# A first attention step whose side work keeps its written place on ScalarE and VectorE, with squares of 1024 columns

## The chip, the cores and the metric

The kernel runs on one core of a Trainium2 chip. The metric is the device time in microseconds (us); the time before is 915.18 us, the median of three runs (911.49 to 916.68). The engines are TensorE (PE; PEld is its weight load), VectorE (DVE), ScalarE (ACT), GpSimd (POOL) and SyncE (SP, which here only issues transfers).

## The reference, cut to what matters

One layer: a normalized input times a weight matrix, neighbourhood attention per head on a grid of 8 by 64 tokens, a gate, a second weight matrix, a second norm and the residual. All is float32, with 512 tokens, width 2048 and 16 heads of 128.

```python
h = rms_norm(x, norm_pre)                 # x * rsqrt(mean(x*x) + eps) * gain
q, k, v, z = split(h @ w_in, 4)           # 2048 -> 4 * 2048
o = neighbourhood_attention(q, k, v, rpb) # windows of 8 x 16 tokens, bias rpb
y = (o * silu(z)) @ w_out
out = x + rms_norm(y, norm_post)
```

## The kernel before, in words

**Precision and products.** Every float32 operand is split into two parts in a format that TensorE takes at full rate: `hi`, a rounding made by ScalarE, and `lo`, the rest, made by VectorE (`split_a` L145 for x, `prep` L231 for a tile of W). A product is hi*hi + lo*hi + hi*lo. A tile of W is 128 rows by 512 columns; it is called tile m here, and its parts `hi`m and `lo`m stand in three buffers each (the pool `wp`).

**Steps.** The product with `w_in` is cut into eight steps of two heads. Step 0 (m from 0 to 31, `mm_first` L260) multiplies plainly: 32 tiles of W with 12 matmuls of 512 columns each. Steps 1 to 7 use seven half-size products in place of eight (a Winograd scheme), whose operands are sums of blocks of x. Those sums are made once, while step 0 runs: `sum_x` (L157) makes four differences of 128x256 on VectorE for each k from 0 to 7, and `split_a` then splits the results into the operands N2 (buffers a`k`_2) and N4 with S1 (buffers a`k`_0, from where step 0 reads its own operands until tile 16+k is done).

**The norm.** The scale of a token, `rc`, is applied to the products of step 0 when they leave PSUM (`take_first` L280), so the squares of x may be summed beside the matmuls. `square_x` (L169) loads x in token order and squares it on ScalarE with a running sum. Before, it does so in 16 pieces of 128x512 that alternate between two buffers, whose tags `bm` and `braw` later hold the bias of the first head. For the first quarter of the tokens a piece is loaded as two halves of 64 rows. `rstd` (L180) turns the sums into `rc` (VectorE, then a power on GpSimd).

**What sets the order.** The program is written as one loop over m: `prep(m+2)` (parts of a W tile, and the loads that its buffers free), then the matmuls of tile m, then what the table `beside` holds for m. A scheduler then orders each engine's instructions; it may move an instruction past others that it does not depend on. What goes through the helper `InOrder` (L52) keeps its written place. Before, only a few transfers of the last stage use it (`sync`). Every engine works through its queue strictly in the order that the scheduler fixed, and an instruction that waits holds up all behind it on that engine. The in-order queue of SP issues the loads of W (four buffers `raw`), of xT, of x for the squares and of T (eight tiles for step 1).

**Due times.** Tile m+3 can be rounded to `hi` only when the matmuls of tile m are done, since there are three buffers; it is due when tile m+3 starts, two tiles later.

Of the kernel before, what the change touches and what calls it, by code (L numbers as in the profile page):

```python
# [10 lines left out]
F32 = mybir.dt.float32  # L11
F32R = mybir.dt.float32r
AF = mybir.ActivationFunctionType
ALU = mybir.AluOpType

P = 128
D = 2048
L = 512
# [5 lines left out]
KT = D // P  # L24
# [17 lines left out]
KH = KT // 2  # L42
SLOTS = NPASS * KH
FIRST = 2 * KT
A11, S1, A12, N2, A22, N4, N3 = range(NPASS)
# [17 lines left out]
@with_exitstack  # L63
def na_block(ctx: ExitStack, tc: tile.TileContext, xT, x, gpre, gpost, w_in, w_out, rpb, mask, out):
    nc = tc.nc
    sync = InOrder(tc, nc.sync)
    PSUM = bass.MemoryType.PSUM
    cp = ctx.enter_context(tc.tile_pool(name="cp", bufs=1))
    wp = ctx.enter_context(tc.tile_pool(name="wp", bufs=3))
# [2 lines left out]
    sp = ctx.enter_context(tc.tile_pool(name="sp", bufs=1))  # L72
# [7 lines left out]
    def pair(name):  # L80
        return ap.tile([P, 2, L], F32, tag="c", name=name, bufs=6)
# [27 lines left out]
    part = cp.tile([P, 4, 4], F32, name="part")  # L109
    ms = cp.tile([P, 4], F32, name="ms")  # L110
# [4 lines left out]
    for k in range(KH):  # L115
        for n, ops in enumerate(((A11, N4, S1), (A12, A22), (N2, N3))):
            t = ag.tile([P, len(ops), 2, 256], F32R, tag=f"a{k}_{n}", name=f"a{k}_{n}")
# [13 lines left out]
    X = {}  # L131
# [10 lines left out]
            X[k] = X["c", kk - kk % 2][:, kk % 2, :]  # L142
        nc.sync.dma_start(X[k], xT[k])

    def split_a(k, src, o):  # L145

        t, i = AT[k, o]
        src = src.rearrange("p (a b) -> p a b", b=256)
        hi, lo = t[:, i : i + 2, 0, :], t[:, i : i + 2, 1, :]
        nc.scalar.copy(hi, src)  # L150
        nc.vector.tensor_tensor(lo, src, hi.bitcast(F32), ALU.subtract)  # L151

    def take_x(k):
        nc.scalar.activation(X[k], X[k], AF.Copy, scale=gcol[:, k : k + 1])
        split_a(k % KH, X[k], A11 if k < KH else A12)

    def sum_x(k):  # L157
        x0, x1 = X[k], X[k + KH]
        h0, h1 = slice(0, 256), slice(256, 512)
        nc.vector.tensor_tensor(x1[:, h1], x0[:, h1], x1[:, h1], ALU.subtract)  # L160
        nc.vector.tensor_tensor(x0[:, h1], x0[:, h0], x0[:, h1], ALU.subtract)
        nc.vector.tensor_tensor(x0[:, h0], x0[:, h0], x1[:, h1], ALU.subtract)
        nc.vector.tensor_tensor(x1[:, h0], x1[:, h0], x0[:, h0], ALU.subtract)


    x_v = x.rearrange("(r c) d -> c r d", c=GRID_W)
    out_v = out.rearrange("(r c) d -> c r d", c=GRID_W)

    def square_x(i):  # L169
        j, n = divmod(i, 4)  # L170
        ns = slice(n * L, (n + 1) * L)
        t = sp.tile([P, L], F32, tag=("bm", "braw")[i % 2], name=f"sq{i}")
        if j == 0:
            nc.sync.dma_start(t[0:64, :], x_v[56:64, :, ns])
            nc.sync.dma_start(t[64:128, :], x_v[0:8, :, ns])
        else:
            nc.sync.dma_start(t, x_v[16 * j - 8 : 16 * j + 8, :, ns])
        return lambda: nc.scalar.activation(t, t, AF.Square, accum_out=part[:, j, n : n + 1])

    def rstd():  # L180
        nc.vector.reduce_sum(ms, part, axis=mybir.AxisListType.X)
        nc.vector.tensor_scalar(ms, ms, 1.0 / D, EPS, ALU.mult, ALU.add)
        nc.gpsimd.tensor_tensor(rc, ms, mhalf, ALU.pow)

# [20 lines left out]
    for i, m in enumerate(seq):  # L205
        e = max(m - 6, seq[i - NRAW] if i >= NRAW else 0)
# [334 lines left out]
    def at(m, f, *args):  # L541
        beside.setdefault(m, []).append(lambda: f(*args))
# [55 lines left out]
    pending = {}  # L598

    def begin(i):  # L600
        pending[i] = square_x(i)

    for i in range(16):
        at(10 + i, begin, i)
        at(12 + i, lambda i=i: pending.pop(i)())
    at(8, lambda: nc.gpsimd.dma_start(mask_sb, mask))
    at(28, rstd)
    for j in range(4):
        at(28 + j, take_first, 0, j)
        at(FIRST - 1, take_first, 1, j)  # L610
    for k in range(KH):
        at(KT - 1 + 2 * k, sum_x, k)
        at(KT + 2 * k, lambda k=k: split_a(k, X[k], N2))
        at(KT + 1 + 2 * k, lambda k=k: split_a(k, X[k + KH], N4))


    ms3 = cp.tile([P, 4], F32, name="ms3")
# [55 lines left out]
    for m in range(-AHEAD, N):  # L673
# [10 lines left out]
        else:  # L684
            n, k = divmod(m - NIN, KT)
# [69 lines left out]
```

## Time and profile before

| | before |
|---|---|
| median of three runs | 915.18 us (911.49 to 916.68) |
| the profiled execution | 915.94 us |
| its span | 914.2 us |
| PE busy | 891.9 us, 98% of the span |
| DVE busy | 690.0 us, 75% |
| ACT busy | 536.7 us, 59% |

Busy shares are means over stages. Step 0 is the first 100 us of the span. A row of a timeline gives the start, the duration, the engine, the line of the kernel, the operation, and in brackets how long the engine had stood idle before it and what ended that.

### The profile page before, as it was taken

The page shows a single profiled execution, that of the slowest core. Times are in us where ns is not written, and L with a number is a line of the kernel's source. Part 1 is how long each engine was busy: PE and PEld are TensorE (multiplying, and loading weights), DVE is VectorE, ACT ScalarE, POOL GpSimd, SP SyncE. Part 2 cuts the span into 40 slices and gives each one's busy share as a digit, 9 for nine tenths or more (in the row PEclk, how much of TensorE's full clock was granted, in tenths as well). Part 3 has the DMA queues.
Part 4 walks back from the last instruction along what each step waited for, and adds up shares of the span by engine and source line. Part 5 has one row for each costly group of instructions (what it writes and reads, how often), then busy time and mean ns, then how long its engine had stood idle before and what let it go on. Part 6 is the DMA issues. An engine that isn't in the chain of part 4 may idle for free.

```text
span 914.2 us, 13095 instructions
## 1 busy us (share of the span) xinstructions
PE 891.9 (98%) x4232; PEld 738.8 (81%) x4232; DVE 690.0 (75%) x1280; ACT 536.7 (59%) x1049; POOL 35.9 (4%) x63
## 2 busy tenths in 40 slices
PE   9989999999999999999999999999999899999995
PEld 8867888888888888888888888878887688888884
DVE  4845679897989889888979897979798755232336
ACT  7855666575758565855675577647675655232322
POOL 0001000000000000000000000000011100000004
PEclk9999999999999999999999999999999999999998
DMA  8884346855784777476747765776588532337635
GB/s 269 234 236 132 106 133 216 255 173 170 228 259 136 219 215 258 109 221 215 256 116 236 217 221 149 225 245 192 156 263 255 162 81 75 110 97 203 175 114 184
DMA packets 91637, 171.72 MB, mean 188 GB/s; under 512 B 10656, under 2 KB 10656, under 8 KB 91568
## 3 DMA queue, kind: packets, MB, share of 16 engines
q1 hardware_dynamic: 87840, 159.95, 56.8%
q0 software_dynamic: 3296, 10.41, 4.3%
q8 instruction: 33, 0.54, 0.2%
q10 hardware_dynamic: 432, 0.53, 0.2%
q14 instruction: 36, 0.29, 0.1%
HBM read 162.98 MB, written 7.86 MB: 187 GB/s over the span
## 4 chain that ended last, share of the span: by engine, by line
PE 61%; issue 20%; DMA 4%; DVE 4%; POOL 1%; ACT 1%; DVEq 0%; POOLq 0%; ACTq 0%
DMA raw<-in_w_in 4%; PE u5Y L299 4%; PE u1Y L299 4%; PE u3Y L299 3%; PE u6Y L299 3%; PE u L278 3%; PE u4Y L299 3%; PE u2Y L299 3%; PE u7Y L299 3%; PE u5X L299 2%; PE u3X L299 2%; PE u6X L299 2%; PE u1X L299 2%; PE u7X L299 2%; PE u2Z L299 2%
## 5 line engine op out<-in xcount | busy, mean ns | idle before, releaser
L242 DVE TENSOR_TENSOR lo<-raw,hi 128x512 fp32r<-128x512 f32 x208 | 142.3, 690 | 153.7 <-ACT hi L241 138.1
L241 ACT CAST hi<-t 128x512 fp32r<-128x512 f32 x280 | 170.7, 617 | 108.9 <-DVE t L238 22.9
L241 ACT CAST hi<-raw 128x512 fp32r<-128x512 f32 x208 | 128.3, 620 | 153.6 <-PE y L640 80.3
L242 DVE TENSOR_TENSOR lo<-t,hi 128x512 fp32r<-128x512 f32 x280 | 190.0, 685 | 11.8 <-ACT hi L241 8.3
L640 PE MATMUL y<-hi,g 128*128 128x512 f32 x512 | 160.3, 393 | 0.6 <-DVE e L341 0.6
L238 DVE TENSOR_TENSOR t<-t,raw 128x512 f32<-128x512 f32 x224 | 150.0, 686 | 10.6 <-DMA raw<-in_w_in 9.8
L640 PEld LDWEIGHTS y<-hi,g 128*128 128x128 f32 x512 | 95.8, 189 | 21.9 <-DVE e L341 1.5
L640 PE MATMUL y<-lo,g 128*128 128x512 f32 x256 | 100.4, 392 | 0.0
L278 PE MATMUL u<-hi,a 128*128 128x512 f32 x256 | 65.0, 392 | 5.3 <-ACT hi L241 5.3
L278 PEld LDWEIGHTS u<-hi,a 128*128 128x128 f32 x256 | 47.6, 188 | 17.1 <-ACT hi L241 7.4
L640 PEld LDWEIGHTS y<-lo,g 128*128 128x128 f32 x256 | 48.3, 189 | 10.1 <-DVE lo L242 0.2
L278 PE MATMUL u<-lo,a 128*128 128x512 f32 x128 | 35.3, 390 | 1.1 <-DVE lo L242 1.1
L151 DVE TENSOR_TENSOR a<-x,a 128x512 fp32r<-128x512 f32 x32 | 21.6, 688 | 13.7 <-ACT a L150 13.5
L278 PEld LDWEIGHTS u<-lo,a 128*128 128x128 f32 x128 | 24.0, 188 | 6.5 <-DVE lo L242 1.5
L348 ACT ACTIVATE s<-s,rc 128x512 f32<-128x512 f32 x28 | 20.1, 719 | 13.4 <-DVE s L335 12.7
L299 PE MATMUL u7Y<-hi,a 128*128 128x512 f32 x96 | 26.9, 397 | 0.4 <-ACT hi L241 0.4
L419 DVE TENSOR_TENSOR bm<-braw,mask_sb 128x256 f32<-128x256 f32 x48 | 27.2, 598 | 0.0
L299 PE MATMUL u2Y<-hi,a 128*128 128x512 f32 x96 | 26.8, 396 | 0.0
L299 PE MATMUL u6Y<-hi,a 128*128 128x512 f32 x96 | 26.8, 396 | 0.0
L299 PE MATMUL u1Y<-hi,a 128*128 128x512 f32 x96 | 26.8, 396 | 0.0
L299 PE MATMUL u3Y<-hi,a 128*128 128x512 f32 x96 | 26.8, 396 | 0.0
L299 PE MATMUL u5Y<-hi,a 128*128 128x512 f32 x96 | 26.8, 396 | 0.0
(400 smaller groups left out, 1792.4 us busy)
## 6 DMA issues: line engine op xcount, KB each, us to landing
raw<-in_w_in SPq DMA_DIRECT2D x368, 256.0 KB, 3.1
t<-in_w_in SPq DMA_DIRECT2D x112, 256.0 KB, 4.1
raw<-in_w_out SPq DMA_DIRECT2D x64, 256.0 KB, 2.6
x<-in_xT SPq DMA_DIRECT2D x16, 256.0 KB, 4.1
spare<-in_x SPq DMA_DIRECT2D x16, 256.0 KB, 3.8
graw<-zm POOLq DMA_DIRECT2D x14, 256.0 KB, 4.1
gr<-graw POOLq DMA_DIRECT2D x14, 256.0 KB, 4.6
out<-spare SPq DMA_DIRECT2D x14, 256.0 KB, 2.9
```

Source lines behind the costliest of these rows:

```text
L151: nc.vector.tensor_tensor(lo, src, hi.bitcast(F32), ALU.subtract)
L238: nc.vector.tensor_tensor(T[k], T[k], src, ALU.add)
L241: nc.scalar.copy(hi, src)
L242: nc.vector.tensor_tensor(lo, src, hi.bitcast(F32), ALU.subtract)
L278: nc.tensor.matmul(U[n][j], l, r, start=k == 0 and i == 0, stop=k == KT - 1 and i == 2)
L299: nc.tensor.matmul(U[c][s], l, r, start=p in (0, 1, 4) and k == 0 and n == 0, stop=k == KH - 1 and n == 2, skip_group_check=True,)
L348: nc.scalar.activation(t[:, s, :], t[:, s, :], AF.Copy, scale=rc[:, j + s : j + s + 1])
L419: nc.vector.tensor_tensor(bm[:, i, :].rearrange("p (a b) -> p a b", b=8), rev, mask_sb[:, i, :].unsqueeze(2).to_broadcast([P, 32, 8]), ALU ...
L640: nc.tensor.matmul(Y[n][t], l[:, tsl], r, start=k == 0 and i == 0, stop=k == KT - 1 and i == 2)
```

## The change

The differences of x (`sum_x`), the splits of the later operands and the squares go through `InOrder` on VectorE and ScalarE, and the loads for the squares through `sync`; so they keep their written place behind `prep` of the same m. The splits of step 0's own operands (`take_x`) do not. A square now covers 1024 columns: 8 pieces in place of 16, loaded six or fewer tiles ahead (at m = 6+2i, squared at m = 12+2i) into buffers of the pool of pairs (tag `c`, six buffers) in place of `bm` and `braw`.

```diff
-    sync = InOrder(tc, nc.sync)
+    sync, dve, act = (InOrder(tc, e) for e in (nc.sync, nc.vector, nc.scalar))
...
-    def split_a(k, src, o):
+    def split_a(k, src, o, scalar=None, vector=None):
...
-        nc.scalar.copy(hi, src)
-        nc.vector.tensor_tensor(lo, src, hi.bitcast(F32), ALU.subtract)
+        (scalar or nc.scalar).copy(hi, src)
+        (vector or nc.vector).tensor_tensor(lo, src, hi.bitcast(F32), ALU.subtract)
...
-        nc.vector.tensor_tensor(x1[:, h1], x0[:, h1], x1[:, h1], ALU.subtract)
+        dve.tensor_tensor(x1[:, h1], x0[:, h1], x1[:, h1], ALU.subtract)
...
     def square_x(i):
-        j, n = divmod(i, 4)
-        ns = slice(n * L, (n + 1) * L)
-        t = sp.tile([P, L], F32, tag=("bm", "braw")[i % 2], name=f"sq{i}")
+        j, n = divmod(i, 2)
+        ns = slice(2 * n * L, 2 * (n + 1) * L)
+        t = pair(f"sq{i}")
...
-            nc.sync.dma_start(t, x_v[16 * j - 8 : 16 * j + 8, :, ns])
-        return lambda: nc.scalar.activation(t, t, AF.Square, accum_out=part[:, j, n : n + 1])
+            sync.dma_start(t, x_v[16 * j - 8 : 16 * j + 8, :, ns])
+        return lambda: act.activation(t, t, AF.Square, accum_out=part[:, j, n : n + 1])
...
-        nc.vector.reduce_sum(ms, part, axis=mybir.AxisListType.X)
+        nc.vector.reduce_sum(ms, part[:, :, 0:2], axis=mybir.AxisListType.X)
...
-    for i in range(16):
-        at(10 + i, begin, i)
-        at(12 + i, lambda i=i: pending.pop(i)())
+    for i in range(8):
+        at(6 + 2 * i, begin, i)
+        at(12 + 2 * i, lambda i=i: pending.pop(i)())
...
-        at(KT + 2 * k, lambda k=k: split_a(k, X[k], N2))
-        at(KT + 1 + 2 * k, lambda k=k: split_a(k, X[k + KH], N4))
+        at(KT + 2 * k, lambda k=k: split_a(k, X[k], N2, act, dve))
+        at(KT + 1 + 2 * k, lambda k=k: split_a(k, X[k + KH], N4, act, dve))
```

The order of TensorE's instructions is the same in both. On the other engines it differs in step 0 and at the start of step 1 only. ScalarE in the second half of step 0, before (`sq` is a square, `hi` the first part of a tile of W, `a` an operand of step 0 or of a later step):

```order
L178 ACTIVATE sq6_585,part_109<-sq6_585 128x512
L241 CAST hi16_516<-raw16_419 128x512
L150 CAST a6_2_131<-x6_260 128x2x256
L178 ACTIVATE sq7_608,part_109<-sq7_608 128x512
L150 CAST a7_2_134<-x6_260 128x2x256
L241 CAST hi17_537<-raw17_445 128x512
L178 ACTIVATE sq8_635,part_109<-sq8_635 128x512
L178 ACTIVATE sq9_658,part_109<-sq9_658 128x512
L241 CAST hi18_562<-raw18_471 128x512
L241 CAST hi19_589<-raw19_498 128x512
```

ScalarE at the same tiles of W, now (L60 is the helper `InOrder`):

```order
L241 CAST hi16_513<-raw16_425 128x512
L60 ACTIVATE sq1_391,part_109<-sq1_391 128x1024
L241 CAST hi17_534<-raw17_450 128x512
L241 CAST hi18_556<-raw18_473 128x512
L60 ACTIVATE sq2_441,part_109<-sq2_441 128x1024
L60 CAST a0_2_113<-x0_147 128x2x256
L241 CAST hi19_583<-raw19_499 128x512
L60 CAST a0_0_111<-x8_305 128x2x256
L241 CAST hi20_607<-raw20_517 128x512
```

Before, two squares could stand ahead of one part of W, and the operands a6_2 and a7_2 were split while tile 16 was prepared; now each part of W comes first, and one or two pieces of side work follow it. VectorE near the start of the program (`lo` is the second part of a tile of W, `bm` the bias of the first head), before:

```order
L242 TENSOR_TENSOR lo4_233<-raw4_168,hi4_232 128x512
L151 TENSOR_TENSOR a3_0_120<-x3_188,a3_0_120 128x2x256
L242 TENSOR_TENSOR lo5_255<-raw5_177,hi5_254 128x512
L151 TENSOR_TENSOR a4_0_123<-x4_215,a4_0_123 128x2x256
L151 TENSOR_TENSOR a5_0_126<-x4_215,a5_0_126 128x2x256
```

And now:

```order
L242 TENSOR_TENSOR lo4_233<-raw4_168,hi4_232 128x512
L419 TENSOR_TENSOR bm0_924<-braw0_922,mask_sb_103 128x256 x2
L151 TENSOR_TENSOR a3_0_120<-x3_188,a3_0_120 128x2x256
L419 TENSOR_TENSOR bm0_924<-braw0_922,mask_sb_103 128x256
L242 TENSOR_TENSOR lo5_255<-raw5_177,hi5_254 128x512
```

The bias of the first head, whose buffers no square uses any more, moved ahead of the fourth and fifth tiles; its load (`braw0`, on GpSimd's queue) now follows the load of the mask there. SP's queue, where the loads of the first square stood behind x10 to x13 (the blocks of xT for tiles 10 to 13), now reads:

```order
L143 DMA x9_328<-in_xT 128x512
L60 DMA sq0_342<-in_x 64x1x1024
L221 DMA raw10_281<-in_w_in 128x512
L60 DMA sq0_342<-in_x 64x1x1024
L221 DMA raw11_303<-in_w_in 128x512
L143 DMA x10_354<-in_xT 128x512
L143 DMA x11_377<-in_xT 128x512
L221 DMA raw12_326<-in_w_in 128x512
```

So x10 and x11 are issued behind raw11, and 512 KB of squares are ahead of them.

## Rows read from the trace of the kernel before

**Rows 1.** Windows of step 0 and of the rest; columns: stretch, length, busy times.

```profile
5.76:46.74 40.98, 40.98 (x181) 33.86 (x182) 29.89 (x60) 32.06 (x60) 0.00 (x0) 1.00 0.83 256
46.74:76.08 29.34, 23.22 (x97) 17.45 (x95) 13.28 (x28) 16.96 (x40) 1.81 (x2) 1.00 0.76 211
78.94:100.70 21.76, 21.76 (x98) 18.02 (x97) 9.72 (x15) 8.06 (x14) 0.58 (x1) 1.00 0.43 119
100.70:914.20 813.50, 798.71 (x3825) 662.87 (x3823) 633.51 (x1174) 473.66 (x928) 31.91 (x50) 0.99 0.61 186
```

**Rows 2.** Timeline of PE in step 0: first matmuls of some tiles of W.

```profile
46.74 0.61 PE L278 MATMUL u<-hi,a 128*128 128x512 f32 x2
...
58.72 2.12 PE L278 MATMUL u<-hi,a 128*128 128x512 f32 x8 [1.40 <-ACT hi L241]
...
76.08 2.11 PE L278 MATMUL u<-hi,a 128*128 128x512 f32 x8 [1.90 <-ACT hi L241]
...
78.94 1.98 PE L278 MATMUL u<-hi,a 128*128 128x512 f32 x8
```

**Rows 3.** Who waited for whom from 46 to 78 us: total, times, longest.

```profile
ACT sq L178 <- DMA sq<-in_x: 11.1, 9, 1.9
...
PE u L278 <- ACT hi L241: 5.0, 4, 1.9
...
ACT c L285 <- POOL rc L183: 1.7, 1, 1.7
```

**Rows 4.** Timeline of ACT before one of PE's stops.

```profile
55.69 0.63 ACT L178 ACTIVATE sq<-sq 128x512 f32<-128x512 f32 x1 [1.42 <-DMA sq<-in_x]
...
57.44 0.63 ACT L178 ACTIVATE sq<-sq 128x512 f32<-128x512 f32 x1 [1.03 <-DMA sq<-in_x]
...
58.07 1.12 ACT L241 CAST hi<-raw 128x512 fp32r<-128x512 f32 x2
```

**Rows 5.** Groups by line, 0 to 115 us: busy, mean ns, idle before.

```profile
L242 DVE TENSOR_TENSOR lo<-raw,hi 128x512 fp32r<-128x512 f32 x32 | 22.0, 690 | 24.1 <-ACT hi L241 17.5 <-PE u L278 6.4 <-issue 0.2
...
L241 ACT CAST hi<-raw 128x512 fp32r<-128x512 f32 x32 | 19.6, 616 | 8.6 <-PE u L278 5.8 <-DMA raw<-in_w_in 2.6
...
L178 ACT ACTIVATE sq<-sq 128x512 f32<-128x512 f32 x16 | 10.1, 631 | 14.8 <-DMA sq<-in_x 14.7
...
L163 DVE TENSOR_TENSOR x<-x,x 128x256 f32<-128x256 f32 x8 | 3.4, 420 | 0.0
...
L178 ACT ACTIVATION_READ_ACCUMULATOR sq<-sq 128x1 f32 x16 | 3.0, 187 | 0.0
```

**Rows 6.** Tile `x`: its loads from issue to landing.

```profile
DMA to landing us min/median/max: 2.9/4.1/6.1
```

**Rows 7.** Timeline of SP: the load that takes the place of x10 now.

```profile
22.32 0.43 SPq L143 DMA_DIRECT2D x<-in_xT  x1
```

**Rows 8.** The window 10 to 20 us, columns as in the first group.

```profile
10.00:20.00 10.00, 10.00 (x46) 8.27 (x45) 6.03 (x10) 8.03 (x15) 0.00 (x0) 1.00 0.90 305
```

**Rows 9.** Timeline of DVE and ACT near the start.

```profile
6.59 0.72 ACT L154 ACTIVATE x<-x,gcol 128x512 f32<-128x512 f32 x1 [0.89 <-DMA x<-in_xT]
...
11.63 0.69 DVE L242 TENSOR_TENSOR lo<-raw,hi 128x512 fp32r<-128x512 f32 x1 [0.16 <-issue]
...
13.36 0.69 DVE L151 TENSOR_TENSOR a<-x,a 128x512 fp32r<-128x512 f32 x1 [1.04 <-ACT a L150]
...
15.63 0.69 DVE L242 TENSOR_TENSOR lo<-raw,hi 128x512 fp32r<-128x512 f32 x1 [1.57 <-ACT hi L241]
```

**Rows 10.** DMA issues from 0 to 100 us: KB, median us to landing.

```profile
braw<-in_rpb POOLq DMA_DIRECT2D x2, 184.0 KB, 3.9
mask_sb<-in_mask POOLq DMA_DIRECT2D x1, 48.0 KB, 4.9
```

**Rows 11.** Timeline at the start of step 1: ACT's parts, PE's third tile.

```profile
101.93 1.14 ACT L241 CAST hi<-t 128x512 fp32r<-128x512 f32 x2
...
103.42 1.07 PE L299 MATMUL u1X<-hi,a 128*128 128x512 f32 x4
```

More of the change, by code (lines that the diff above doesn't have):

```diff
@@ L159, in sum_x @@
         h0, h1 = slice(0, 256), slice(256, 512)
-        nc.vector.tensor_tensor(x1[:, h1], x0[:, h1], x1[:, h1], ALU.subtract)
-        nc.vector.tensor_tensor(x0[:, h1], x0[:, h0], x0[:, h1], ALU.subtract)
-        nc.vector.tensor_tensor(x0[:, h0], x0[:, h0], x1[:, h1], ALU.subtract)
-        nc.vector.tensor_tensor(x1[:, h0], x1[:, h0], x0[:, h0], ALU.subtract)
+        dve.tensor_tensor(x1[:, h1], x0[:, h1], x1[:, h1], ALU.subtract)
+        dve.tensor_tensor(x0[:, h1], x0[:, h0], x0[:, h1], ALU.subtract)
+        dve.tensor_tensor(x0[:, h0], x0[:, h0], x1[:, h1], ALU.subtract)
+        dve.tensor_tensor(x1[:, h0], x1[:, h0], x0[:, h0], ALU.subtract)
     x_v = x.rearrange("(r c) d -> c r d", c=GRID_W)
@@ L169, in square_x @@
     def square_x(i):
-        j, n = divmod(i, 4)
-        ns = slice(n * L, (n + 1) * L)
-        t = sp.tile([P, L], F32, tag=("bm", "braw")[i % 2], name=f"sq{i}")
+        j, n = divmod(i, 2)
+        ns = slice(2 * n * L, 2 * (n + 1) * L)
+        t = pair(f"sq{i}")
         if j == 0:
-            nc.sync.dma_start(t[0:64, :], x_v[56:64, :, ns])
-            nc.sync.dma_start(t[64:128, :], x_v[0:8, :, ns])
-        else:
-            nc.sync.dma_start(t, x_v[16 * j - 8 : 16 * j + 8, :, ns])
-        return lambda: nc.scalar.activation(t, t, AF.Square, accum_out=part[:, j, n : n + 1])
+            sync.dma_start(t[0:64], x_v[56:64, :, ns])
+            sync.dma_start(t[64:128], x_v[0:8, :, ns])
+        else:
+            sync.dma_start(t, x_v[16 * j - 8 : 16 * j + 8, :, ns])
+        return lambda: act.activation(t, t, AF.Square, accum_out=part[:, j, n : n + 1])
     def rstd():
-        nc.vector.reduce_sum(ms, part, axis=mybir.AxisListType.X)
+        nc.vector.reduce_sum(ms, part[:, :, 0:2], axis=mybir.AxisListType.X)
         nc.vector.tensor_scalar(ms, ms, 1.0 / D, EPS, ALU.mult, ALU.add)
```

## The prediction

> **What bounds the kernel now.** I looked first at the busy shares, where PE is busy for 98% of the span, so only PE's gaps can be won back. The windows tell where they are [rows 1]: from 78.94 to 100.70 us PE takes the last eight tiles of step 0 in 21.76 us, which is 2.72 us for a tile without a gap. The first fifteen tiles (5.76 to 46.74) take 40.98 us, 0.18 more than 15 x 2.72. The eight tiles from 46.74 to 76.08 take 29.34 us where 8 x 2.72 is 21.76: there 7.58 us are lost, and 0.14 more in the next tile (76.08 to 78.94 [rows 2]). That makes 7.72 us that step 0 loses after its fifteenth tile. In the 813.5 us behind step 0 PE stands idle for 14.8, but the order of the instructions there is the same in both kernels, and I leave that as it is.
>
> The waits between 46 and 78 us name the cause [rows 3]: PE waited for `hi` 5.0 us in four stops, and ScalarE itself waited nine times, 11.1 us in all, for the loads of squares. The timeline shows the link [rows 4]: two squares in a row stand ahead of `hi`18, the first waits 1.42 us for its transfer, the second 1.03, then `hi` is cast at 58.07, and at 58.72 PE starts after 1.40 us of idleness [rows 2]. The squares come late because two buffers carry all sixteen: a load can go out only when the square two earlier is done. Loads of W are not the cause: over the first 115 us ScalarE waited for them 2.6 us [rows 5].
>
> **The change part by part.** *The eight pieces on ScalarE.* Six buffers are in reach, and a load is issued six tiles (16.3 us) ahead, where loads of x land after 4.1 us in the median and 6.1 at most [rows 6]. From the third square on, loads have more than 10 us to land. If one is late all the same, `hi` behind it has a margin: it may start when tile m-3 is done and is due 5.44 us later; less its own 0.62 and a square that is 4.2 us are left for wait and side work. I cost the squares' waits at nothing, and the whole 7.72 us come back. A square of 1024 columns lasts at least the 0.63 us of one of 512 and at most twice that, 1.26, and 0.19 to read the sum [rows 5]; eight take at most 11.6 us where sixteen take 13.1. That is off the path either way.
>
> *The sums and later operands.* In a pair of tiles VectorE makes two `lo` (0.69 each), four differences (0.42 each) and two subtractions of operands, which last like a `lo`: 4 x 0.69 + 4 x 0.42 = 4.44 us [rows 5], of the 5.44 that PE takes for the pair. ScalarE makes four casts of 0.62 and a square: 2.48 + 1.45 = 3.9 us of 5.44. So each engine is done before its next part of W can start. The new places add waits: a cast of N2 waits for the differences, and behind it on ScalarE stands the `hi` of the next tile. But the differences come right behind the `lo` of the tile before and end at most 0.69 + 0.69 + 4 x 0.42 = 3.1 us after the `hi` of that tile, and the cast has a whole `hi` and a square ahead of it. Nothing is lost here; if this cover is gone, the excess over 5.44 us falls on each of eight pairs.
>
> *The loads of the first square, now ahead of x10 and x11.* x10 takes x13's old place behind raw11, issued at 22.32 us [rows 7], and x11 goes out 0.43 later, at about 22.8. With the longest landing, 6.1 us [rows 6], it is there at 28.9. Tile 10 starts at 5.76 + 0.18 + 10 x 2.72 = 33.14; before that ScalarE has to scale x11, split it and cast `hi`10, some 2 us, so x11 is due at 31.2. The margin is 2.3 us, the cost nothing; if x11 comes at 33, it is 1.8 us. Later blocks have more room, except x15, which stands ahead of `hi`14 on ScalarE.
>
> By the Trainium skill (DMA: Bandwidth & Descriptors, "Why a DMA increments its semaphore by 16 and not by 1") a transfer is split over the largest number of engines, up to 16, that divides the slowest dimension on both sides; the halves of 64 rows read a slowest dimension of 8, so they would use 8 engines. No row here shows how many engines they use. By it the 512 KB of the first square would hold back what follows like 1 MB, 1.7 us more at 305 GB/s [rows 8]: x11 would be there at 30.6 and its margin be 0.6 us. The sum would stay, and that is one reason why the rival of a late x has the chance below.
>
> *The bias of the first head, now early.* Its load (184 KB) follows the mask's on GpSimd's queue, issued near 2.5 us into a full set of transfers. At the 305 GB/s of the busiest window [rows 8] it takes 0.6 us. The scaling of x1 waited 0.89 us for its load at 6.59 [rows 9], and PE starts on x1 as soon as it is scaled and split, so that place has no slack I can count on: the cost is between 0 and 0.6 us. I take 0.3, the middle, as part of the bytes go out behind x1. On VectorE three biases of 0.6 us stand where it idled 1.04 and 1.57 us [rows 9]: two of them from 12.3 to 13.5 us, the third behind a3. With a landing of 3.9 us, as for this load later, or 4.9 as for the mask [rows 10], the load is there before 8 us, and they cost nothing. They wait in the queue in front of a3 and `lo`5, so a landing after 14 us would stop PE.
>
> *The end of step 0.* The cast and the subtraction of the last N4 now stand ahead of `hi`34 and `lo`34. `hi`34 starts at 101.93 and its tile at 103.42 [rows 11]: 1.49 us, of which a cast takes 0.52 from start to start (1.14 - 0.62) and `hi`34 itself 0.62. It fits by 0.3 us; bounds 0 and 0.6 (one cast late), I take 0.1. `rc` now comes late: between `hi`28 and `hi`29 stand the eighth square (1.45), a cast (0.62), the wait for `rc` (1.7 before [rows 3]) and two readers of it, which I estimate like casts (1.24). That is 5.0 us where 2.1 would be in step, so `hi`29 is 2.9 us late, inside its 4.8 (5.44 - 0.62): nothing.
>
> **Sum.** 7.72 - 0.3 - 0.1 = 7.3 us. Against the profiled execution (915.94, its span 914.2 and 1.74 around it) that is 908.6. This execution lies 0.76 above the median of 915.18; from the median it would be 907.9. I say 908.2.
>
> **The rivals.**
> 1. *A late x or a late bias keeps part of the stops.* Between 20 and 45 us the squares' loads now go before x10 to x15, in a stretch where transfers already set when x is scaled, and each x stands ahead of a `hi` on ScalarE. For it: the waits for x and the margin of 2.3 us. Against it: PE has no stop there before. Price: one or two stops like those of before, 1.4 to 1.9 us each [rows 2], so 2 to 4 us: 910.5 to 912.5.
> 2. *The transfers were the bound.* The 4 MB of squares still have to come while T and W are loaded, at DMA shares of 0.76 to 0.83 [rows 1]; then `raw` is late in place of the square, PE's stops move to it, and at most 2 us come back: 913 to 915. Against it: 2.6 us of waits for W, and 211 GB/s in the stretch with the stops beside 305 in another.
> 3. *The fixed order makes a round trip, and the kernel is slower.* If VectorE and ScalarE do not overlap (cast waits for the differences, subtraction for the cast, the next `hi` for both), a pair of tiles takes ScalarE's and VectorE's work in a row, 3.9 + 4.4 = 8.3 us in place of 5.44, and eight pairs lose 23 us: 915.9 - 7.3 + 23 = 931.6. It decides from 5.44 + 7.3/8 = 6.35 us per pair. For it: these instructions can no longer be moved past a wait. Against it: the order puts a part of W between every two of them, and neither engine's own work passes 4.5 us.
> 4. *The order changes nothing that PE feels*, because the stops come from elsewhere: excluded as far as the rows go, since the stops of PE end on `hi` and stand right behind the squares' waits; it would give 914 to 916.
>
> **How the numbers follow.** Forecast 0.70, rival 1 0.13, rival 2 0.10, rival 3 0.05, rival 4 0.02. A measurement of this kernel can tell about 0.5%, 4.6 us, from no change, so faster means below 910.6. The three runs of before spread over 5 us, so I take 0.03 from the forecast to "same"; rival 1 falls half on each side. Faster: 0.67 + 0.07 = 0.74; same: 0.03 + 0.06 + 0.10 + 0.02 = 0.21; slower 0.05. The range goes down to 905, the forecast less the 3 us that the fastest run of before lies under its median, and up to 913, which takes in rival 1.
>
> **What would show it.** In the profile after, PE's tiles 15 to 23 come every 2.72 us, step 1 starts near 93.3 us in place of 100.70, ScalarE's wait for squares is under 2 us in all, and the first bias is added before 15 us. Step 0 ending early while the rest of the span grows would show a gain given back. A wait of ScalarE for x10 to x15 with a stop of PE behind it speaks for rival 1, `hi` waiting for `raw` for rival 2, VectorE or ScalarE idle in each pair for the other, with PE's tiles over 2.72 us, for rival 3. Wrong I would be also if PE reached its fourth tile after 15 us, behind a late bias.

## The result, and the profile after

The changed kernel takes 909.08 us in the median of 19 runs (905.51 to 915.58), the kernel before, run beside it, 914.40 (19 runs, 909.53 to 919.40). The ratio is 0.9949, with a 95% interval of 0.9931 to 0.9968, so some 4.7 us. The profiled execution took 907.16 us, its span 905.4. In a second comparison it took 911.49 us, a ratio of 0.9969 (0.9948 to 0.9990). The forecast was 908.2 us with a range of 905 to 913, and faster was to mean below 910.6: the first median is, the second is not. Both intervals lie below 1, so the kernel is faster in both, by little.

Windows after, columns as in [rows 1]: the first thirteen tiles, the stretch that held the stops, the last eight tiles of step 0, and steps 1 to 7.

```profile
6.04:42.80 36.76, 35.80 (x160) 29.30 (x158) 18.70 (x30) 23.71 (x40) 0.54 (x1) 1.00 0.87 266
...
45.65:72.99 27.34, 27.34 (x121) 22.64 (x121) 20.61 (x39) 18.25 (x34) 0.00 (x0) 1.00 0.99 258
72.99:94.75 21.76, 21.76 (x97) 18.02 (x96) 16.75 (x34) 14.25 (x25) 1.57 (x1) 1.00 0.33 95
...
94.75:706.86 612.11, 610.44 (x2969) 509.05 (x2968) 544.78 (x1018) 400.33 (x778) 20.59 (x38) 1.00 0.65 203
```

From 45.65 to 72.99 us PE is busy throughout: ten tiles in 27.34 us, where 10 x 2.72 is 27.2. The eight tiles with the stops took 29.34 before [rows 1]. Step 1 starts at 94.75 us, 5.95 earlier than at 100.70. From there to the last stage it is 612.11 us here and 612.50 before (100.70 to 713.20), so nothing is given back in steps 1 to 7.

The timeline of PE after, at its start and at the one later hitch:

```profile
6.04 2.09 PE L278 MATMUL u<-hi,a 128*128 128x512 f32 x8
...
9.99 2.12 PE L278 MATMUL u<-hi,a 128*128 128x512 f32 x8 [0.96 <-ACT a L150]
...
12.87 1.30 PE L278 MATMUL u<-hi,a 128*128 128x512 f32 x5
...
45.65 2.12 PE L278 MATMUL u<-hi,a 128*128 128x512 f32 x8
...
94.75 1.07 PE L299 MATMUL u1X<-hi,a 128*128 128x512 f32 x4
```

The second tile comes 3.95 us after the first where 2.72 are due, and the third 2.88 after the second. ScalarE's and GpSimd's timelines show why:

```profile
8.06 0.72 ACT L154 ACTIVATE x<-x,gcol 128x512 f32<-128x512 f32 x1 [2.42 <-DMA x<-in_xT]
```

```profile
1.54 0.70 POOL L606 DMA_DIRECT2D mask_sb<-in_mask  x1
2.24 0.56 POOL L413 DMA_DIRECT2D braw<-in_rpb  x1
```

The scaling of x1 starts at 8.06 us after a wait of 2.42, where it was 6.59 after 0.89 [rows 9]: 1.47 us later. The bias load is issued at 2.24 us, among the first loads of x and W.

The waits of the first 96 us after (columns as in [rows 3]) and the groups by line of the first 115 (as in [rows 5]):

```profile
ACT x L154 <- DMA x<-in_xT: 13.8, 10, 4.0
...
ACT hi L241 <- DMA raw<-in_w_in: 3.6, 4, 1.6
...
ACT c L285 <- POOL rc L183: 1.7, 1, 1.7
...
PE u L278 <- ACT a L150: 1.0, 1, 1.0
```

```profile
L242 DVE TENSOR_TENSOR lo<-raw,hi 128x512 fp32r<-128x512 f32 x32 | 21.8, 689 | 13.8 <-ACT hi L241 12.6 <-DMA x<-in_xT 0.9
...
L60 ACT ACTIVATE sq<-sq 128x1024 f32<-128x1024 f32 x8 | 8.5, 1057 | 0.0
...
L60 ACT ACTIVATION_READ_ACCUMULATOR sq<-sq 128x1 f32 x8 | 1.5, 185 | 0.0
```

The squares wait for nothing, where they waited 14.7 us [rows 5], and PE's waits show no stop on `hi`. ScalarE waits for x instead, 13.8 us; PE feels little of it (the second tile, and 0.27 us around tile 14). The DMA issues of the first 100 us (columns as in [rows 10]):

```profile
raw<-in_w_in SPq DMA_DIRECT2D x38, 256.0 KB, 3.7
x<-in_xT SPq DMA_DIRECT2D x16, 256.0 KB, 4.6
sq<-in_x SPq DMA_DIRECT2D x6, 512.0 KB, 8.7
...
braw<-in_rpb POOLq DMA_DIRECT2D x2, 184.0 KB, 5.6
```

### The profile page after: what moved, and what is told of

Same layout as the page of the kernel before. It is cut to its first block, busy times and chain, and to the rows that moved or that the text cites. A ratio compares the mean times of both kernels' runs of the same rounds, so it can differ in the third digit from the quotient of the medians.

```text
span 905.4 us, 13034 instructions
## 1 busy us (share of the span) xinstructions
PE 890.0 (98%) x4232; PEld 739.0 (82%) x4232; DVE 692.0 (76%) x1280; ACT 535.9 (59%) x1033; POOL 36.2 (4%) x63
## 4 chain that ended last, share of the span: by engine, by line
PE 70%; issue 20%; DVE 4%; DMA 3%; POOL 1%; ACT 1%; SPq 0%; DVEq 0%; POOLq 0%; ACTq 0%
PE u L278 9%; PE u6Y L299 4%; PE u4Y L299 4%; PE u1Y L299 3%; PE u3Y L299 3%; PE u5Y L299 3%; PE u2Y L299 3%; PE u7Y L299 2%; PE u3X L299 2%; PE u7X L299 2%; PE u5X L299 2%; PE u4X L299 2%; PE u1X L299 2%; PE u6X L299 2%; PE u6Z L299 2%
## 5 line engine op out<-in xcount | busy, mean ns | idle before, releaser
L299 PE MATMUL u4Y<-hi,a 128*128 128x512 f32 x96 | 26.8, 396 | 0.0
```

Of the source, the lines that this page charges most:

```text
L299: nc.tensor.matmul(U[c][s], l, r, start=p in (0, 1, 4) and k == 0 and n == 0, stop=k == KH - 1 and n == 2, skip_group_check=True,)
```

## The experiments

E is the start of step 1 in a trace: 100.70 us before, 94.75 after. Each ratio is to the kernel before in runs on the same chip.

**The bias load (e1_bias_late).** After, with the load of the first bias moved to tile 24, on SP's queue.

```diff
-        nc.gpsimd.dma_start(raw[:, 0 : 7 * TBL + 32], src)
+        (sync if h == 0 else nc.gpsimd).dma_start(raw[:, 0 : 7 * TBL + 32], src)
...
-        at(when(h, 0) - (4 if late else 11), load_bias, h)
+        at(24 if h == 0 else when(h, 0) - (4 if late else 11), load_bias, h)
```

> The changed kernel, with the load of the first head's bias moved from GpSimd's queue at the start to SP's queue behind the loads of tile 24's step. Theory: the 184 KB of the bias, in flight at 2.2 us, held back x1 (scaled at 8.06 us after a wait of 2.42, where it was 6.59 and 0.89). Then x1 is scaled near 6.6, the second tile starts near 8.6 and step 1 near 93.4 us in place of 94.75; the time falls by 1.3 us to about 907.8, a ratio to the kernel before of 0.9935. Rival: the late x1 is chance of that execution; then step 1 starts at 94 to 95 us and the ratio stays at 0.995.

Measured: 910.11 us in 6 runs, ratio 0.9939 (0.9918 to 0.9961); E 93.14, 1.61 earlier than after. PE's second tile starts at 8.82 and has no stop:

```profile
5.99 2.09 PE L278 MATMUL u<-hi,a 128*128 128x512 f32 x8
7.92 1.07 PE L278 MATMUL u<-lo,a 128*128 128x512 f32 x4
8.82 1.98 PE L278 MATMUL u<-hi,a 128*128 128x512 f32 x8
```

PE's third tile starts at 11.54 where after has 12.87, so the early load cost the start 1.33 us; the rest of the 1.61 is the hitch around tile 14. x1 is scaled at 5.52 without a wait, earlier than the 6.6 expected. From step 1 to the last stage, though, this trace takes 613.94 us where after took 612.11. Run again beside a repeat of after:

> The changed kernel once more. Theory (the early load of the bias holds back x1 in every execution): x1 is scaled after 7.5 us again, PE's second tile starts at 9.5 us or later and step 1 at 94.2 us or later. Rival (chance): the second tile starts before 9.0 us.

> The changed kernel with the late bias once more, on the chip of the changed kernel. Theory: the second tile starts before 9.4 us, step 1 at 93 to 93.8 us, and the median lies 0.5 to 2 us under that of the changed kernel. Rival: no difference in time, since what is won at the start is lost again in step 1 to 7 (the first execution took 613.9 us from step 1 to the last stage where the changed kernel took 612.1).

Measured: after 911.49 us (12 runs, ratio 0.9969), E 94.83, its second tile at 10.36 behind a stop of 1.45 us; the late bias 909.06 (6 runs, ratio 0.9937, 0.9914 to 0.9959), E 92.91. One expectation failed: x1 was not scaled after 7.5 us but at 5.61, without a wait. What came late in the repeat was tile 1 of W, in ScalarE's timeline:

```profile
5.61 0.72 ACT L154 ACTIVATE x<-x,gcol 128x512 f32<-128x512 f32 x1
9.17 0.62 ACT L241 CAST hi<-raw 128x512 fp32r<-128x512 f32 x1 [2.84 <-DMA raw<-in_w_in]
```

So the early load goes with a late second tile of PE in both traces, but it is not always x1 that is late. E differs by 1.6 and 1.9 us in the two pairs of traces; steps 1 to 7 take 1.83 and 0.51 us more with the late bias (613.94 against 612.11, 613.14 against 612.63), for reasons that stay open. The ratios (0.9949 against 0.9939, then 0.9969 against 0.9937) point the same way, but their intervals overlap: a gain in the whole time is not shown.

**The early load in the kernel before (e6_early_load_in_before).** One load of the same size and place, into a buffer that is free then.

```diff
+    spare_src = bass.AP(rpb.tensor, rpb.offset, [[1, 16], [TBL, 8], [1, 7 * TBL + 32]])
+    at(8, lambda: nc.gpsimd.dma_start(T[7][:, 0 : 7 * TBL + 32], spare_src))
```

> The kernel before with one more load of 184 KB on GpSimd's queue right behind the mask's, into a tile that nothing reads before its own load; everything else in the same order. Theory (an early load of this size holds back x1): the scaling of x1 moves from 6.59 to about 8 us and the second tile of PE from 8.61 to about 10. Rival (chance): both stay within 0.3 us of the kernel before. The end of step 0 may not move, as the squares set the pace there.

Measured in one run: 917.15 us, E 102.53; a repeat of before (below) has E 102.76, so E tells nothing here (both traces hold a fall of the granted clock, told at the end), but the start does. ScalarE's and PE's timelines:

```profile
7.62 0.72 ACT L154 ACTIVATE x<-x,gcol 128x512 f32<-128x512 f32 x1 [2.05 <-DMA x<-in_xT]
9.79 0.62 ACT L241 CAST hi<-raw 128x512 fp32r<-128x512 f32 x1 [1.44 <-DMA raw<-in_w_in]
```

```profile
10.97 3.44 PE L278 MATMUL u<-hi,a 128*128 128x512 f32 x8 [2.34 <-ACT a L150]
```

With the load alone, and nothing of the change, ScalarE scales x1 1.03 us later than in before (6.59 [rows 9]) and then waits 1.44 us for tile 1 of W; PE stops for 2.34 ahead of its second tile. Over all thirteen traces the second tile starts at 9.99 to 10.97 us in the four that have this load at the start (after, its repeat, e3 and e6) and at 8.59 to 9.53 in the nine that do not.

**The order alone (e2_order_alone).** Before, with all of the change's `InOrder`, but sixteen squares of 512 columns in the two old buffers.

```diff
-    sync = InOrder(tc, nc.sync)
+    sync, dve, act = (InOrder(tc, e) for e in (nc.sync, nc.vector, nc.scalar))
...
-        return lambda: nc.scalar.activation(t, t, AF.Square, accum_out=part[:, j, n : n + 1])
+        return lambda: act.activation(t, t, AF.Square, accum_out=part[:, j, n : n + 1])
```

> The kernel before with sums, later operands and squares kept in their written place, but with the sixteen squares of 512 columns in the two old buffers. Theory (the loop of the two buffers makes the stops): a square's load can go out only when the square two earlier is done, so a pair takes a landing of 4.3, an issue of 0.6 and a square of 0.8, 5.7 us or more against the 5.44 of two tiles; ScalarE still waits for squares over 5 us in all and step 1 starts at 96 to 100 us; ratio 0.996 to 1.0. Rival (the place behind the parts of W alone removes the stops, since a hi then waits for one square at most): step 1 starts below 95 us, ratio 0.995 or lower.

Measured: 908.97 us (5 runs), ratio 0.9930 (0.9914 to 0.9945); E 93.66, no stop of PE in step 0. The squares still wait, 5.9 us in six stops, but no part of W is late for it. My theory that two buffers made the squares late fell here; the rival, that their place decides, held.

**The larger squares alone (e3_squares_alone).** After, with sums, operands and squares free again; the loads keep their order, the six buffers stay.

```diff
-        return lambda: act.activation(t, t, AF.Square, accum_out=part[:, j, n : n + 1])
+        return lambda: nc.scalar.activation(t, t, AF.Square, accum_out=part[:, j, n : n + 1])
...
-        at(KT + 2 * k, lambda k=k: split_a(k, X[k], N2, act, dve))
+        at(KT + 2 * k, lambda k=k: split_a(k, X[k], N2))
```

> The changed kernel with the sums, later operands and squares free to move again; only the squares of 1024 columns in the pair buffers and their loads in written order are left. Theory (the loop of the two buffers made the stops): ScalarE waits for squares under 2 us in all, step 1 starts at 94 to 96 us as in the changed kernel, ratio 0.994 to 0.997. Rival (the written place makes the gain): squares and sums again stand ahead of parts of W, PE stops behind them by over 3 us, step 1 starts at 98 us or later, ratio 0.998 to 1.001.

Measured: 916.66 us (12 runs), ratio 1.0017 (0.9997 to 1.0037); E 101.44. SP's, ScalarE's and PE's timelines around one stop:

```profile
54.83 0.55 SPq L60 DMA_DIRECT2D sq<-in_x  x1
```

```profile
59.88 1.06 ACT L178 ACTIVATE sq<-sq 128x1024 f32<-128x1024 f32 x1 [3.52 <-DMA sq<-in_x]
60.84 0.19 ACT L178 ACTIVATION_READ_ACCUMULATOR sq<-sq 128x1 f32 x1
60.94 1.12 ACT L241 CAST hi<-raw 128x512 fp32r<-128x512 f32 x2
```

```profile
61.59 2.51 PE L278 MATMUL u<-hi,a 128*128 128x512 f32 x8 [1.91 <-ACT hi L241]
```

A square's load goes out at 54.83, and the square begins 5.05 us later; the scheduler put it (the fifth) ahead of `hi`18, where the changed kernel has it behind `hi`22. ScalarE waits 3.52 us in front of it, then casts `hi`18, and PE has stood idle for 1.91. Six buffers don't help a square that stands five tiles too early: the squares' waits are 17.5 us, more than before.

**One kind of side work at a time (e7, e8).** Both start from e1. e7 frees sums and operands and pins the squares; e8 frees the squares and pins the rest.

```diff
# e7, against e1
-        dve.tensor_tensor(x1[:, h1], x0[:, h1], x1[:, h1], ALU.subtract)
+        nc.vector.tensor_tensor(x1[:, h1], x0[:, h1], x1[:, h1], ALU.subtract)
...
-        at(KT + 2 * k, lambda k=k: split_a(k, X[k], N2, act, dve))
+        at(KT + 2 * k, lambda k=k: split_a(k, X[k], N2))
# e8, against e1
-        return lambda: act.activation(t, t, AF.Square, accum_out=part[:, j, n : n + 1])
+        return lambda: nc.scalar.activation(t, t, AF.Square, accum_out=part[:, j, n : n + 1])
```

> The kernel with the late bias, but with only the squares kept in their written place; the sums and later operands are free to move. Theory now (a free square stands two to four tiles of W early on ScalarE, ahead of a hi, and waits there for its load): with the squares behind hi22 and later nothing waits in front of a hi, step 1 starts below 94.5 us and PE has no stop over 0.5 us after its second tile; ratio 0.992 to 0.996. Rival (the sums and operands that move ahead also hold up hi and lo): PE stops stay, step 1 starts at 96 us or later.

> The kernel with the late bias, but with the sums and later operands kept in their written place and the squares free. Theory now: the squares stand early again (the fourth ahead of hi15, the fifth ahead of hi18), ScalarE waits for them over 10 us in all, PE stops behind them and step 1 starts at 97 to 101 us; ratio 0.997 to 1.001. Rival (either part of the order is enough): step 1 starts below 95 us.

Measured: e7 910.71 us (7 runs), ratio 0.9942 (0.9918 to 0.9966), E 94.40, one stop of 0.16 us at 45.09. e8 919.19 us (10 runs), ratio 1.0041 (1.0020 to 1.0061), E 105.25, both beyond what was expected. ScalarE and PE in e8:

```profile
57.95 1.06 ACT L178 ACTIVATE sq<-sq 128x1024 f32<-128x1024 f32 x1 [6.35 <-DMA sq<-in_x]
58.91 0.19 ACT L178 ACTIVATION_READ_ACCUMULATOR sq<-sq 128x1 f32 x1
59.00 1.12 ACT L241 CAST hi<-raw 128x512 fp32r<-128x512 f32 x2
```

```profile
59.66 2.12 PE L278 MATMUL u<-hi,a 128*128 128x512 f32 x8 [3.08 <-ACT hi L241]
```

The squares' place carries the gain, and it alone. With sums and operands fixed and the squares free, the squares move up further and wait 21.9 us, up to 6.35 at a time: this version is slower than before. Not all of that is stops in step 0: behind one of them the granted clock fell (told at the end), and steps 1 to 7 take 616.65 us, 4.15 more than before, and why stays open.

**The smallest edit (e10_only_squares_pinned).** Before, with the squares on ScalarE through `InOrder` and nothing else: sixteen squares, two buffers, free sums, free loads.

```diff
-    sync = InOrder(tc, nc.sync)
+    sync, act = (InOrder(tc, e) for e in (nc.sync, nc.scalar))
...
-        return lambda: nc.scalar.activation(t, t, AF.Square, accum_out=part[:, j, n : n + 1])
+        return lambda: act.activation(t, t, AF.Square, accum_out=part[:, j, n : n + 1])
```

> The kernel before with one edit alone: the sixteen squares keep their written place on ScalarE. Theory (only the place of the squares matters): PE has no stop over 0.5 us in step 0 after the second tile, step 1 starts at 93 to 94.5 us, ratio 0.991 to 0.996. Rival (the two small buffers or the free sums bring stops back): step 1 starts at 96 us or later, ratio 0.997 or more.

Measured: 909.31 us (6 runs), ratio 0.9932 (0.9908 to 0.9956); E 92.92, 7.78 us earlier than before, span 904.1. Its timeline of ScalarE, and step 0 as one window:

```profile
51.77 0.60 ACT L241 CAST hi<-raw 128x512 fp32r<-128x512 f32 x1
54.00 0.63 ACT L60 ACTIVATE sq<-sq 128x512 f32<-128x512 f32 x1 [1.62 <-DMA sq<-in_x]
...
55.14 0.61 ACT L241 CAST hi<-raw 128x512 fp32r<-128x512 f32 x1
```

```profile
5.70:92.92 87.22, 87.22 (x385) 72.18 (x385) 55.92 (x105) 60.19 (x118) 2.19 (x3) 1.00 0.73 224
```

PE has no gap in 87.22 us, 0.18 over 32 x 2.72. A square waits 1.62 us for its transfer and delays nothing, since the `hi` ahead of it is already cast and the next is not due. Two lines give the whole gain of the change, and nothing here shows this kernel to be slower than the changed one (909.31 beside 915.89 for before, a ratio of 0.9932 where the changed kernel has 0.9949 and 0.9969).

**Later squares (e4_late_bias_late_squares).** e1 with the squares' loads two tiles later, to see whether the order of the loads makes ScalarE wait for x.

```diff
-        at(6 + 2 * i, begin, i)
+        at(8 + 2 * i, begin, i)
```

> The kernel with the late bias, with the loads of the squares issued two tiles later (at m = 8+2i). Theory (the squares' loads ahead of x10 and x11 lengthen the waits for x): ScalarE's waits for x fall from 8 to 10 us with the late bias to below 6, while step 1 still starts at 92.8 to 93.4, as no stop of PE comes from them. Rival (x waits come from the total of the transfers, not from their order): the waits for x stay above 7 us.

Measured in one run: 909.04 us, E 93.88. The waits for x stay at 11.3 us (9.9 in e1), so this order of the loads does not make them; nor does the loads' total by itself, as e2 and e10 load the same bytes and wait 4.4 and 3.5 us for x. What makes them stays open. The squares now wait 3.1 us, and PE stops once in step 0, 0.47 us at 42.03, and once in step 1, 0.62 us for a `hi` at 97.38. A miss for the theory, and no gain.

**The kernel before, once more (before_again).**

> The kernel before once more. Theory (free squares make the stops in every execution): four or five stops of PE behind squares, step 1 starts at 99 to 102 us; the seven steps from there take 612 to 614 us. If the gain in time is less than the 5.9 us of the traces because the stops differ between executions, step 1 starts below 99 us here.

Measured in one run: 918.10 us, E 102.76, six stops of PE between 48 and 77 us, the first on `lo` and five on `hi` (0.56, 0.34, 0.70, 1.28, 1.17 and 2.00 us), 14.9 us of waits for squares. The stops belong to the kernel, not to one execution. They sum to 6.05 us where the first trace has 6.12; E is 2.06 later mainly because PE, behind the last stop, takes 4.44 us for a tile (76.56 to 81.00) where the first trace takes 2.86, at a lower granted clock:

```profile
76.56 3.42 PE L278 MATMUL u<-hi,a 128*128 128x512 f32 x8 [2.00 <-ACT hi L241]
```

```profile
76.56:79.98 3.42, 3.42 (x9) 2.72 (x10) 3.42 (x7) 3.42 (x7) 0.30 (x1) 0.57 0.31 77
```

The column 0.57 is the granted clock; it is 1.00 behind the same stop of the first trace (1.90 us at 76.08). Steps 1 to 7 take 612.74 us, as in the first trace (612.50).

## Why the prediction was right

**Where the time was, and that the order gives it back: right.** The 7.72 us of stops are gone from the trace after, and in e10 with the one edit that the theory needs; `hi` behind a waiting square was the cause. E moved by 5.95 us, against 7.3 forecast.

**The 0.3 us for the early bias: mis-sized.** I took the load's share of the bandwidth, 0.6 us, as the upper bound. Measured were 1.47 us at the scaling of x1, 1.2 more lost by PE at its second and third tile (1.23 + 0.16, less the 0.18 of before), and 1.6 and 1.9 us in E against the late bias. The step that failed is "the cost is between 0 and 0.6 us": a load beside others delayed what PE needs for its second tile by more than its own bytes take. I had only x1 in view; in the repeat of after x1 was in time and tile 1 of W was late, with the same effect on PE. The bias itself was there in time (added at 13.74 us, before 15); PE reached its fourth tile at 15.60 us, after the 15 that I had named, but behind x1.

**"If x11 comes late": nearly.** x10 and x11 were issued from 24.86 us on, not 22.8, and x11 was scaled at 30.38 without a wait. To the 31.2 that I had worked out that leaves 0.8 us, not 2.3. By luck PE was itself 1.5 us late (tile 10 started at 34.64, not 33.14), which gave the difference back. Later x cost PE 0.27 us around tile 14 (45.65 to the tile after), all that came of the first rival; the repeat of after has no such hitch. The landing was also taken too short: the 512 KB of a square landed after 8.7 us in the median, not the 4.1 of x, and the 16.3 us of six tiles covered it. So 7.72 − 1.2 − 0.27 is 6.2 us, and the first matmul was 0.28 later: 5.95. That last 0.28 is within what the first tile's start varies by (5.62 to 6.20 us in these traces).

**"The squares come late because two buffers carry all sixteen": wrong.** e3 has six buffers and is no faster; e2 and e10 have two and keep the whole gain. What decides is where the square stands on ScalarE. The eight larger pieces, costed at nothing, are worth nothing either: their 1.06 + 0.19 us make 10.0 where sixteen took 13.1, off the path.

**Sums and operands, `rc`, the end of step 0, costed at 0 to 0.1 us: right.** PE's tiles come every 2.72 us from 51.23 to 94.75, so `hi`29 behind the late `rc` cost nothing, and the first tiles of step 1 keep their 1.36 us, so `hi`34 behind a cast cost nothing either. That margin is thin all the same: in e4, where the cast of the last operand also stands ahead (at 96.20 us), PE's third tile of step 1 stopped for 0.62 us on `hi`, the upper bound that I had given. e7 and e10 leave them free and e2 pins them, with E between 92.92 and 94.40.

**The other rivals.** Transfers were not the bound: after, the DMA share is 0.99 from 45.65 to 72.99 us, and PE does not wait. No round trip: the tiles keep 2.72 us.

**From 5.95 us to the 4.7 measured, and the 8.8 of the two profiled spans.** The span gains 5.95 in step 0, 0.39 in steps 1 to 7, and 2.46 behind 706.86 us. Of those 2.46, 1.79 are PE's last stage, which comes and goes in one kernel too (see the end). The 5.95 lie inside the interval of the first comparison (2.9 to 6.3 us) and above that of the second (0.9 to 4.8). Between the two repeats E differs by 7.93 us (102.76 and 94.83), 1.6 of it by the lower clock behind the last stop of before. Nothing of it is given back in steps 1 to 7 (612.74 and 612.63). Single runs of one kernel scatter over 10 us, and why the median gains 1 to 5 us less than step 0 does in these traces stays open.

## What to carry to other kernels

On an engine that works strictly in order, side work that waits for a transfer must stand behind the work that the bound engine needs, not ahead of it: fix that place first, and only then think of buffers and piece sizes. When freed buffers let another load start earlier, look at what else is in flight at that moment; at the start of a program its price is the delay of the loads that PE waits for, and here that was two to three times what its own bytes take. And undo a change part by part: here one of its four parts had the whole gain, one cost the start 1.3 to 1.9 us, and the rest nothing that can be seen.

## What the runs showed of the hardware

A load of 184 KB issued at 2.2 us on GpSimd's queue delayed loads of 256 KB on SP's, though at 305 GB/s [rows 8] it takes 0.6 us: x1 was scaled 1.47 us later in after and 1.03 in e6 than in before, and tile 1 of W, which is cast at 6.33 to 7.61 us in the nine traces without the load, was cast at 8.80 to 9.79 in the four with it: in after it stood behind the late x1, in the repeat of after, e3 and e6 ScalarE waited 2.84, 2.66 and 1.44 us for its load. Which load is late differs between executions of one kernel.

Squares of 1024 columns took 1.06 us, of 512 0.63: 0.43 us for 512 columns more.

The granted clock fell behind some stops of PE and not behind others. In step 0 a stop of 2.00 us (the repeat of before), of 2.34 (e6, at 10.97) and of 3.80 (e8, at 83.34) was followed by a tile of 4.44, 4.44 and 5.29 us where 2.72 are due, at a granted clock of 0.57, 0.56 and 0.50 in its first 3.4 to 3.8 us; behind 1.91 us (e3, at 61.59) the tile took 4.01. Behind 1.90 us (before, at 76.08) and 3.08 (e8, at 59.66) the clock stayed at 1.00, and the tiles took 2.86 and 2.87. So a stop can cost another 1.3 to 2.6 us beyond its own length. In the other nine traces the clock of step 0 is 1.00 throughout.

Behind a stop of PE in the last stage (1.55 to 2.50 us, for an operand of head 14) the granted clock fell in 6 of 13 traces for about 5 us, in others not, in the same kernel too. Windows of the same stretch, in before, in the repeat of after, and in after:

```profile
728.20:733.20 5.00, 5.00 (x22) 4.25 (x22) 3.00 (x10) 3.57 (x10) 0.00 (x0) 0.70 0.09 33
```

```profile
722.46:727.46 5.00, 5.00 (x20) 4.15 (x19) 3.77 (x15) 3.78 (x10) 0.00 (x0) 0.66 0.02 9
```

```profile
721.86:726.86 5.00, 5.00 (x27) 4.25 (x26) 4.14 (x16) 4.29 (x13) 0.00 (x0) 1.00 0.05 14
```

The column behind the busy times is the granted clock, a mean over the window of its two levels (1.00 is 2.4 GHz, half of it 1.2). The matmuls in 5 us are 20 to 22 where it fell and 27 where it held. Before it PE had stood idle for 2.17, 1.81 and 1.99 us: the three stops differ little, so these rows do not tell why one kept its clock. PE's last stage takes 190.8 to 191.4 us where it falls and 189.1 to 189.8 where not: some 1.7 us that are in before's profiled span and not in after's, by chance.
